# Column sums of squares accumulated by the matrix engine in the RMS norms of the third block, with four fillers ahead of the mixer

## The chip, the core and the metric

The kernel runs on one core of one Trainium2 chip. Its engines work beside each other, each through its own queue in order: the matrix engine (TensorE; PE for matmuls and PEld for weight loads in the profile), the vector engine (VectorE, DVE), the scalar engine (ScalarE, ACT), GpSimd (POOL), and SyncE (SP), which issues most of the transfers. The metric is the time of one execution on the device in microseconds (us); lower is better. Times of the profile are measured from the first instruction of the profiled execution.

## What is computed

One step of a two-layer streaming encoder, 1024 prompt positions and 64 sample positions, model width 1024, all in float32. Each layer has a mixer (layer 0: windowed attention with sinks; layer 1: a complex diagonal state-space mixer, S5, with a GLU) and a convolutional FFN of width 2816. Each of the four parts has an RMS norm ahead of it and one behind it:

```
def rms_norm(x, g):
    x32 = x.astype(jnp.float32)
    y = x32 * lax.rsqrt(jnp.mean(x32 * x32, axis=-1, keepdims=True) + NORM_EPS) * g.astype(jnp.float32)
    return y.astype(x.dtype)

for i in range(DEPTH):
    hp = rms_norm(xp, g_pre_mix[i])
    ...                                   # mixer: mp from hp
    xp = xp + rms_norm(mp, g_post_mix[i])
    hp = rms_norm(xp, g_pre_ffn[i])
    fp, cpi = conv_ffn(hp, ...)
    xp = xp + rms_norm(fp, g_post_ffn[i])
```

The sample rows (`xs`) go the same way.

## The kernel before

Activations lie transposed: the 1024 features are 8 groups (`k`) of 128 partitions, the 1088 positions are columns, cut into three blocks of 384, 384 and 320 (`BLK`; b = 0, 1, 2). Large matmuls are done as three passes of a split operand (`mm3`, lines 223 to 225: low part times high weights, high times high, high times low). Weights come from HBM as units (`raw`), are split by the scalar and vector engines (`whl`, lines 193/194 and 216) and used in a fixed order.

A norm needs, for each column, the sum of squares over all 1024 features. `rstd` (line 237) does it: the scalar engine squares two groups at a time into a buffer named by its tag (`sqa` or `sqb`, two buffers here; line 254), the vector engine adds these pairs into the first one (`acc`, line 256), then the two halves of the pair (line 260). A matmul with that 128-column piece as weights and a column of ones (scaled by 1/1024) as the moving operand then sums over the partitions, once for each of three column groups of 128 (line 266). Each such float32 matmul appears in the profile as two passes, a load and a matmul each. From the three sums the scalar engine takes a root (line 270), the vector engine a reciprocal and one Newton step (lines 271, 272, 289 to 291), and transposes on the matrix engine spread the result over the partitions (line 284). With `fine` set, which is so for the third block of a norm behind a part, the last pair is squared in two halves (line 248) and each half is added by itself (line 249).

`post_norm` (line 311 on) is the norm behind a part: squares of `y`, scaling of `y` by the gain on the scalar engine (line 320), multiplication by the spread result (line 328), addition of the residual `xl` (line 331). It runs four times for each block: behind attention (post=1), FFN 0 (post=3), the S5 mixer (post=5) and FFN 1 (post=7). Behind post=1 and post=5 follows `pre_norm`, whose outputs `hh` and `hl` (lines 300, 303 to 306) feed the FFN.

Between FFN 0 and the S5 mixer the third block takes another way, in `ssm_norm` (line 1145 on). The transposed mixer input is written to HBM unscaled (`ssm_bounce`: copies `xs` on line 1131, transfers `hd` on line 1137), read back as `U` (line 1186), and scaled later (line 1194) by `rs`, which `ssm_norm` makes of the norm's result: selection matmuls (line 1173) and two copies (lines 1175, 1176). While the squares of that block are made, the matrix engine multiplies an identity matrix by 512 columns of constants whose result nobody reads (`fill`, line 230): eight such fillers, chained by `order` one behind the other and behind the transposes of the norm before. One more filler follows the column sums and one the selection. The copies of groups 2 and 3 are ordered behind the last square.

```
            self.fill(idle, 8, 512, self.last_tr)
        ps, r = self.rstd(xt, n, "sqa" if b == 2 else "sqb", True, bcast=b < 2, ...)
```

The mixer works through 32 pairs of state groups. For each it loads parameters (`pm`, line 1213), multiplies `U` by them (lines 1249 and 1309), turns the results by `sc` (line 1257) and scans on the vector engine (lines 1280 to 1301).

The order of the instructions on each engine isn't the order in which the program issues them: a planner simulates the time line with its own costs and picks, among what is ready, what was issued first. `order(x, first)` adds an edge to it without a semaphore; `later` lowers the priority.

Of the kernel before, what the change touches and what calls it, by code (L numbers as in the profile page):

```python
# [11 lines left out]
AF = mybir.ActivationFunctionType  # L12
# [3 lines left out]
P = 128  # L16
# [27 lines left out]
class Core:  # L44
# [86 lines left out]
    sq = {}  # L131
# [79 lines left out]
    behind = ()  # L211
# [22 lines left out]
        return x  # L234


    def rstd(self, src, n, tag, root, bcast=True, first=False, alt=None, adder=None, fine=False):
        nc = self.nc
        adder = adder or nc.vector
        acc = None  # L240
        for q in range(4):
            sq = self.n2(n, tag)
            xq = src[:, 2 * q:2 * q + 2]
            if fine and q == 3:

                adder.tensor_add(acc[:, 0], acc[:, 0], acc[:, 1])
                for j in range(2):
                    nc.scalar.activation(sq[:, j], xq[:, j], AF.Square)
                    adder.tensor_add(acc[:, 0], acc[:, 0], sq[:, j])
                break  # L250
            if first:
                nc.gpsimd.tensor_mul(sq, xq, xq)
            else:
                self.sq[q] = nc.scalar.activation(sq, xq, AF.Square)
            if q:
                adder.tensor_add(acc, acc, sq)
            else:
                acc = sq
        else:
            adder.tensor_add(acc[:, 0], acc[:, 0], acc[:, 1])  # L260
        cuts = [min(c, n - P) for c in range(0, n, P)]
        nt = len(cuts)
        pr = self.sm_ps("pr", int(tag == "sqb") if alt is None else alt)
        st = pr[:, 384:384 + nt]
        for i, c in enumerate(cuts):
            self.last_st = nc.tensor.matmul(st[:, i:i + 1], acc[:, 0, c:c + P], self.ones, start=True, stop=True)
        v = self.small.tile([P, 4, 4], F32, name="nv" + tag, bufs=3)
        x, hx, r, t = (v[:, i, :nt] for i in range(4))
        if root:
            nc.scalar.activation(x, st, AF.Sqrt, bias=self.eps)  # L270
            nc.vector.tensor_scalar(hx, st, 1e-6, -0.5, op0=ALU.add, op1=ALU.mult)
            nc.vector.reciprocal(r, x)
            self.refine(r, t, hx)
        else:

            nc.vector.tensor_scalar(x, st, 1e-6, None, op0=ALU.add)
            ri = r.bitcast(I32)
            nc.vector.tensor_scalar(ri, x.bitcast(I32), 1, None, op0=ALU.logical_shift_right)
            nc.vector.tensor_scalar(hx, x, -0.5, None, op0=ALU.mult)
            nc.vector.tensor_scalar(ri, ri, -1.0, float(MAGIC), op0=ALU.mult, op1=ALU.add)  # L280
            for _ in range(3):
                self.refine(r, t, hx)
        for i, c in enumerate(cuts if bcast else []):
            self.last_tr = nc.tensor.transpose(pr[:, c:c + P], r[:, i:i + 1].to_broadcast([P, P]), self.ident)
        return pr, r
# [25 lines left out]
    def post_norm(self, y, b, g, xsrc, root, roomy, out=None, by=None):  # L311

        nc = self.nc
        n = BLK[b][1]
        xs = [self.t4([P, 2, n], "xl") if roomy and b == 2 else self.n2(n, "xl") for _ in range(4)]
        for q in range(4):
            nc.sync.dma_start(xs[q], xsrc[:, 2 * q:2 * q + 2])
        pr, _ = self.rstd(y, n, "sqa", root, alt=b % 2 if roomy else None, fine=b == 2)
        for k in range(KD):
            nc.scalar.activation(y[:, k], y[:, k], AF.Copy, scale=g[:, k:k + 1])  # L320
        V, G = nc.vector, nc.gpsimd
        by = [(G, V)[int(x)] for x in by or ("1001" if roomy and b == 2 else "0101")]

        def apply():
            last = None
            for q in range(4):
                yq = y[:, 2 * q:2 * q + 2]
                x = V.tensor_mul(yq, yq, pr[:, None, :n].to_broadcast([P, 2, n]))  # L328
                if last is not None and b == 2:
                    self.order(x, last)  # L330
                x = by[q].tensor_add(yq, yq, xs[q])  # L331
                if by[q] is V:
                    last = x
                if out is not None:
                    nc.sync.dma_start(out[:, 2 * q:2 * q + 2], yq)
        return apply
# [808 lines left out]
    def ssm_norm(self, xt, b):  # L1145

        nc = self.nc
        n = BLK[b][1]
        if b == 2:
            idle = self.mm_ps("idle")  # L1150
            self.fill(idle, 8, 512, self.last_tr)
        ps, r = self.rstd(xt, n, "sqa" if b == 2 else "sqb", True, bcast=b < 2, alt=1 - b % 2, adder=nc.gpsimd if b == 0 else None)
        if b == 0:
            jp = self.t4([P, P], "jp", I32)
            nc.gpsimd.iota(jp, pattern=[[1, P]], base=1, channel_multiplier=1)
            sel = self.t4([P, 1001], "sel")
            self.lsel, self.dsel, self.ex, self.rs, self.rn = (sel[:, x:y] for x, y in ((0, 128), (128, 144), (144, 192), (192, 233), (233, 1001)))
            nc.vector.tensor_scalar(jp, jp, 7, None, op0=ALU.bitwise_and)
            nc.vector.tensor_scalar(self.lsel, jp, 0.0, None, op0=ALU.is_equal)
            dj = self.t4([P, 16], "dj", I32)  # L1160
            nc.gpsimd.iota(dj, pattern=[[-8, 16]], base=0, channel_multiplier=1)
            nc.vector.tensor_scalar(dj, dj, 3, None, op0=ALU.arith_shift_right)
            nc.vector.tensor_scalar(self.dsel, dj, 0.0, None, op0=ALU.is_equal)
            nc.vector.memset(self.rs[:, 32:33], 0.0)
        if b < 2:
            nc.scalar.activation(self.rn[:, 384 * b:384 * b + 384], ps[:, :n], AF.Copy)
            return
        ex = self.ex
        self.fill(idle, 1, 512, self.last_st)
        for i, c in enumerate(range(0, n, P)):  # L1170
            c = min(c, n - P) // 8
            nc.vector.tensor_scalar(ex[:, 16 * i:16 * i + 16], self.dsel, r[:, i:i + 1], None, op0=ALU.mult)
            x = nc.tensor.matmul(ps[:, c:c + 16], self.lsel, ex[:, 16 * i:16 * i + 16], start=True, stop=True)
        self.fill(idle, 1, 256, x)
        nc.scalar.activation(self.rs[:, 0:32], ps[:, :32], AF.Copy)
        self.last_rs = nc.scalar.activation(self.rs[:, 33:41], ps[:, 32:40], AF.Copy)
# [423 lines left out]
```

## Time and profile before

| | |
|---|---|
| median of 3 runs | 2259.78 us (2258.66 to 2261.68) |
| the profiled execution | 2264.88 us, of which the span is 2263.1 us |
| mean granted TensorE clock | 0.990 |
| busy share of the span: PE, PEld, DVE, ACT, POOL | 97%, 94%, 75%, 45%, 18% |
| third block's norm at post=1, post=3, post=5, post=7: column sums start | 385.75, 1186.45, 1518.88, 2250.59 us |
| column sums of `ssm_norm`, third block | 1199.22 us |
| first matmul of the mixer | 1204.04 us |

In the views, a row of a time line gives start, duration, engine, line, operation, `out<-in`, form and count, and in brackets the idle time of the engine before it with what ended it. Rows of the same kind that follow each other are merged, so that a duration then covers the count behind the x.

### The profile page before, as it was taken

How to read it: one execution, taken by the hardware profiler on the slowest of the kernel's cores; microseconds unless marked ns; L12 is line 12 of the kernel's file. 1: busy time of each engine (PE TensorE's matmuls, PEld its weight loads, DVE VectorE, ACT ScalarE, POOL GpSimd, SP SyncE). 2: the span in 40 equal slices, each digit the busy share in tenths (PEclk: the TensorE clock that was granted, in tenths of full speed). 3: DMA queues.
4: the chain of work that ended last, by engine and by line, in shares of the span. 5: the costliest groups of instructions: out<-in, count | busy, mean ns of one | idle time of the engine just before them, and what ended most of it. 6: DMA issues, size and time to landing. Idle time of an engine off the chain costs nothing. (4 is left out here: it accounts for less than half of the span.)

```text
span 2263.1 us, 36074 instructions
## 1 busy us (share of the span) xinstructions
PE 2201.7 (97%) x13875; PEld 2122.4 (94%) x13875; DVE 1688.5 (75%) x2954; ACT 1019.2 (45%) x1839; POOL 415.2 (18%) x474
## 2 busy tenths in 40 slices
PE   8999999999999999999998899999999999999997
PEld 8987789999999999999996799999999999989997
DVE  8677647989877777667767855588997787686764
ACT  5255747422333343455534641263544444355543
POOL 5322004200042423000200034352011011100000
PEclk9999999999999999999998999999999999999999
DMA  5100014656345565887749888652266577578773
GB/s 195 37 21 29 16 65 151 242 191 211 107 138 185 178 203 179 259 288 222 227 164 339 262 286 300 234 166 74 96 233 218 213 287 258 193 250 278 222 256 99
DMA packets 208124, 428.48 MB, mean 189 GB/s; under 512 B 23312, under 2 KB 114224, under 8 KB 205008
## 3 DMA queue, kind: packets, MB, share of 16 engines
q1 hardware_dynamic: 175648, 326.56, 44.0%
q0 software_dynamic: 23984, 95.12, 11.6%
q10 hardware_dynamic: 8320, 4.49, 0.9%
q8 instruction: 109, 1.79, 0.3%
q14 instruction: 63, 0.52, 0.1%
HBM read 297.75 MB, written 128.37 MB: 188 GB/s over the span
## 5 line engine op out<-in xcount | busy, mean ns | idle before, releaser
L223 PE MATMUL mm<-hl,whl 128*128 128x384 f32 (+1 forms) x1960 | 643.8, 329 | 7.7 <-DVE hl L306 3.1
L225 PE MATMUL mm<-hh,whl 128*128 128x384 f32 (+1 forms) x1960 | 641.1, 328 | 2.3 <-DVE whl L216 2.3
L224 PE MATMUL mm<-hh,whl 128*128 128x384 f32 (+1 forms) x1960 | 642.2, 328 | 0.0
L223 PEld LDWEIGHTS mm<-hl,whl 128*128 128x128 f32 x1960 | 368.4, 188 | 10.8 <-DVE hl L306 4.5
L225 PEld LDWEIGHTS mm<-hh,whl 128*128 128x128 f32 x1960 | 368.4, 188 | 2.9 <-DVE whl L216 2.9
L224 PEld LDWEIGHTS mm<-hh,whl 128*128 128x128 f32 x1960 | 368.7, 188 | 0.0
L216 ACT ACTIVATE whl<-raw 128x1024 fp32r<-128x1024 f32 x202 | 212.9, 1058 | 339.1 <-PE mm L225 176.4
L216 DVE TENSOR_TENSOR whl<-raw,whl 128x1024 fp32r<-128x1024 f32 x202 | 254.4, 1263 | 96.7 <-ACT whl L216 96.2
L223 PE MATMUL mm<-gt,whl 128*128 128x384 f32 (+1 forms) x968 | 318.5, 329 | 7.9 <-DVE y L613 3.6
L225 PE MATMUL mm<-gt,whl 128*128 128x384 f32 (+1 forms) x968 | 316.9, 328 | 0.7 <-DVE whl L216 0.7
L224 PE MATMUL mm<-gt,whl 128*128 128x384 f32 (+1 forms) x968 | 317.3, 328 | 0.0
L223 PEld LDWEIGHTS mm<-gt,whl 128*128 128x128 f32 x968 | 182.9, 189 | 10.5 <-DVE y L613 4.9
L225 PEld LDWEIGHTS mm<-gt,whl 128*128 128x128 f32 x968 | 182.7, 189 | 1.0 <-DVE whl L216 1.0
L224 PEld LDWEIGHTS mm<-gt,whl 128*128 128x128 f32 x968 | 182.8, 189 | 0.0
L194 DVE TENSOR_TENSOR whl<-raw,whl 128x1024 fp32r<-128x1024 f32 x84 | 96.3, 1153 | 73.0 <-ACT whl L193 72.4
L193 ACT ACTIVATE whl<-raw 128x1024 fp32r<-128x1024 f32 x84 | 82.6, 986 | 126.8 <-DMA raw<-sd 51.0
L419 ACT ACTIVATE t<-u,ppt 128x1090 f32<-128x1090 f32 x88 | 114.2, 1298 | 50.6 <-DVE u L521 24.6
L420 DVE SCALAR_TENSOR_TENSOR t<-u,ppt,t 128x1090 f32<-128x1090 f32 x88 | 123.6, 1406 | 9.8 <-ACT t L419 9.1
L421 DVE SCALAR_TENSOR_TENSOR t<-u,ppt,t 128x1090 f32<-128x1090 f32 x88 | 123.4, 1403 | 0.4
L563 DVE TENSOR_TENSOR gt<-gr,gt 128x768 fp32r<-128x768 f32 (+2 forms) x106 | 90.2, 880 | 10.7 <-ACT gt L562 10.1
L331 POOL TENSOR_TENSOR y<-y,xl 128x768 f32<-128x768 f32 (+1 forms) x16 | 31.3, 1954 | 354.0 <-DVE y L328 288.0
L562 ACT ACTIVATE gt<-gr 128x768 fp32r<-128x768 f32 (+2 forms) x106 | 78.3, 771 | 39.5 <-DMA gr<-gd 30.2
(390 smaller groups left out, 4181.0 us busy)
## 6 DMA issues: line engine op xcount, KB each, us to landing
raw<-in_w_up SPq DMA_DIRECT2D x88, 512.0 KB, 4.3
raw<-in_w_down SPq DMA_DIRECT2D x74, 512.0 KB, 4.5
raw<-sd SPq DMA_DIRECT2D x40, 512.0 KB, 4.6
sj<-in_w_up POOLq DMA_DIRECT2D x68, 256.0 KB, 6.4
su<-sj POOLq DMA_DIRECT2D x34, 512.0 KB, 5.8
raw<-su SPq DMA_DIRECT2D x34, 512.0 KB, 4.8
pm<-prm SPq DMA_DIRECT2D x32, 522.0 KB, 8.2
gr<-td SPq DMA_DIRECT2D x40, 384.0 KB, 5.9
```

The source lines that it names most:

```text
L193: nc.scalar.activation(w[:, 0], raw, AF.Copy)
L194: nc.vector.tensor_sub(w[:, 1], raw, w[:, 0].bitcast(F32))
L216: x = nc.scalar.activation(w[:, 0], raw, AF.Copy), nc.vector.tensor_sub(w[:, 1], raw, w[:, 0].bitcast(F32))
L223: nc.tensor.matmul(out, w[:, 0, sl], xl, start=start, stop=False)
L224: nc.tensor.matmul(out, w[:, 0, sl], xh, start=False, stop=False)
L225: self.last_mm = nc.tensor.matmul(out, w[:, 1, sl], xh, start=False, stop=stop)
L331: x = by[q].tensor_add(yq, yq, xs[q])
L419: nc.scalar.activation(t, u[:, 0:T + 2], AF.Identity, bias=cb(m), scale=cw(0, m))
L420: nc.vector.scalar_tensor_tensor(t, u[:, 1:T + 3], cw(1, m), t, op0=ALU.mult, op1=ALU.add)
L421: self.last_conv = nc.vector.scalar_tensor_tensor(t, u[:, 2:T + 4], cw(2, m), t, op0=ALU.mult, op1=ALU.add)
L562: nc.scalar.activation(x[:, 0, u], raw, AF.Copy)
L563: nc.vector.tensor_sub(x[:, 1, u], raw, x[:, 0, u].bitcast(F32))
```

## The change

`rstd` takes `late`, a number of pairs, instead of `fine`. Pairs from `late` on aren't added by the vector engine: each 128 x 320 half of their squares goes to the matrix engine by itself, which accumulates the column sums in PSUM over several matmuls (`total`; the first one alone sets the start flag, the last one alone the stop flag). `late=4` is the old way. `late=3` (third block of each `post_norm`) adds the first seven groups on the vector engine as before, sums them on the matrix engine behind the last large matmul (`last_mm`), and then sums the square of the eighth group: six matmuls for three column groups instead of three. `late=0` (third block in `ssm_norm`) makes no adds at all: 24 matmuls instead of three. The PSUM tile `pr` is now taken ahead of the squares. The fillers ahead of that norm become four.

```diff
--- before.py
+++ after.py
@@ -234,20 +234,38 @@
         return x
 
 
-    def rstd(self, src, n, tag, root, bcast=True, first=False, alt=None, adder=None, fine=False):
+    def rstd(self, src, n, tag, root, bcast=True, first=False, alt=None, adder=None, late=4):
+
         nc = self.nc
         adder = adder or nc.vector
         acc = None
+        cuts = [min(c, n - P) for c in range(0, n, P)]
+        nt = len(cuts)
+        pr = self.sm_ps("pr", int(tag == "sqb") if alt is None else alt)
+        st = pr[:, 384:384 + nt]
+
+        def total(x, start, stop, behind=None):
+            for i, c in enumerate(cuts):
+                self.last_st = nc.tensor.matmul(st[:, i:i + 1], x[:, c:c + P], self.ones, start=start and i == 0, stop=stop and i == nt - 1)
+                if behind is not None:
+                    self.order(self.last_st, behind)
         for q in range(4):
             sq = self.n2(n, tag)
             xq = src[:, 2 * q:2 * q + 2]
-            if fine and q == 3:
-
-                adder.tensor_add(acc[:, 0], acc[:, 0], acc[:, 1])
+            if q >= late:
+                if q < 3:
+                    self.sq[q] = nc.scalar.activation(sq, xq, AF.Square)
                 for j in range(2):
-                    nc.scalar.activation(sq[:, j], xq[:, j], AF.Square)
-                    adder.tensor_add(acc[:, 0], acc[:, 0], sq[:, j])
-                break
+                    if q == 3:
+                        self.sq[q] = nc.scalar.activation(sq[:, j], xq[:, j], AF.Square)
+                    if late == 3 and j == 0:
+
+                        adder.tensor_add(acc[:, 0], acc[:, 0], acc[:, 1])
+                        adder.tensor_add(acc[:, 0], acc[:, 0], sq[:, j])
+                        total(acc[:, 0], True, False, self.last_mm)
+                    else:
+                        total(sq[:, j], q + j == 0, q + j == 4)
+                continue
             if first:
                 nc.gpsimd.tensor_mul(sq, xq, xq)
             else:
@@ -256,14 +274,9 @@
                 adder.tensor_add(acc, acc, sq)
             else:
                 acc = sq
-        else:
+        if late == 4:
             adder.tensor_add(acc[:, 0], acc[:, 0], acc[:, 1])
-        cuts = [min(c, n - P) for c in range(0, n, P)]
-        nt = len(cuts)
-        pr = self.sm_ps("pr", int(tag == "sqb") if alt is None else alt)
-        st = pr[:, 384:384 + nt]
-        for i, c in enumerate(cuts):
-            self.last_st = nc.tensor.matmul(st[:, i:i + 1], acc[:, 0, c:c + P], self.ones, start=True, stop=True)
+            total(acc[:, 0], True, True)
         v = self.small.tile([P, 4, 4], F32, name="nv" + tag, bufs=3)
         x, hx, r, t = (v[:, i, :nt] for i in range(4))
         if root:
@@ -315,7 +328,7 @@
         xs = [self.t4([P, 2, n], "xl") if roomy and b == 2 else self.n2(n, "xl") for _ in range(4)]
         for q in range(4):
             nc.sync.dma_start(xs[q], xsrc[:, 2 * q:2 * q + 2])
-        pr, _ = self.rstd(y, n, "sqa", root, alt=b % 2 if roomy else None, fine=b == 2)
+        pr, _ = self.rstd(y, n, "sqa", root, alt=b % 2 if roomy else None, late=3 if b == 2 else 4)
         for k in range(KD):
             nc.scalar.activation(y[:, k], y[:, k], AF.Copy, scale=g[:, k:k + 1])
         V, G = nc.vector, nc.gpsimd
@@ -1148,8 +1161,9 @@
         n = BLK[b][1]
         if b == 2:
             idle = self.mm_ps("idle")
-            self.fill(idle, 8, 512, self.last_tr)
-        ps, r = self.rstd(xt, n, "sqa" if b == 2 else "sqb", True, bcast=b < 2, alt=1 - b % 2, adder=nc.gpsimd if b == 0 else None)
+            self.fill(idle, 4, 512, self.last_tr)
+        ps, r = self.rstd(xt, n, "sqa" if b == 2 else "sqb", True, bcast=b < 2, alt=1 - b % 2, adder=nc.gpsimd if b == 0 else None,
+                          late=0 if b == 2 else 4)
         if b == 0:
             jp = self.t4([P, P], "jp", I32)
             nc.gpsimd.iota(jp, pattern=[[1, P]], base=1, channel_multiplier=1)
```

## The prediction

> **What bounds the kernel now.** I read the page first, then the chain of waits at the end, then the time line at the four places where the third block (320 columns) is normed, and the windows of the matrix engine's clock.
>
> ```profile
> span 2263.1 us, 36074 instructions
> PE 2201.7 (97%) x13875; PEld 2122.4 (94%) x13875; DVE 1688.5 (75%) x2954; ACT 1019.2 (45%) x1839; POOL 415.2 (18%) x474
> ```
> ```profile
> L266 PEld LDWEIGHTS pr<-ones,sqa x78: 186/192/192, 346.1 to 2251.1; 128*128 128x128 f32 x78
> ```
>
> The matrix engine is busy 97% of the span: what the edit can win lies in the 61 us where it isn't, and work put on it costs time wherever it is dense. The row by tile is a norm's column sum: 78 loads in 13 norms, so six passes a norm, two for each of three column groups. The profiled execution took 2264.88 us, 5.1 above the median of 2259.78 of the runs; I sum against the execution and carry the difference over to the median.
>
> The chain of waits at the kernel's end:
>
> ```profile
> 2248.93 0.50 DVE y L657
> 2249.45 0.48 ACT sqa L248
> 2249.95 0.50 DVE sqa L249
> 2250.59 0.81 PE pr L266 x6
> 2251.43 0.27 ACT nvsqa L270
> ```
>
> After the last matmul all is serial: last add, square of the last k, its add into the partial sum (L249), six passes, root. Nothing there hides a step.
>
> **The change, part by part.** *Last norm (post=7).* Removed is the second L249; the passes start behind the square. Added are six passes for the partial sum, ahead of it. Six loads take
>
> ```profile
> 2250.56 0.74 PEld L266 LDWEIGHTS pr<-ones,sqa 128*128 128x128 f32 x6 [1.93 <-issue]
> ```
>
> with 0.19 for a single one (192 ns above), so a further pass adds (0.74 - 0.19) / 5 = 0.11 us, and six in a stream 0.67. The partial sum's are ordered behind the last matmul, over by 2248.93, and the last square ends at 2249.93: 1.0 us of idle engine covers 0.74 of passes; without that cover up to 0.74 would be paid. The gain is L249's row, -0.5; bounds -0.5 and +0.2.
>
> *Norm ahead of the mixer (post=3).* The same edit, but the scalar engine stands in between:
>
> ```profile
> 1185.81 0.49 DVE L249 TENSOR_TENSOR sqa<-sqa 128x320 f32<-128x320 f32 x1 [0.63 <-ACT sqa L248]
> ```
> ```profile
> 1185.33 0.45 ACT L248 ACTIVATE sqa<-y 128x320 f32<-128x320 f32 x1
> 1186.18 0.53 ACT L1257 ACTIVATE sc<-pm 128x138 f32<-128x138 f32 x2 [0.40 <-DMA pm<-prm]
> 1186.62 0.55 ACT L320 ACTIVATE y<-y,ppt 128x320 f32<-128x320 f32 x1
> 1187.29 0.26 ACT L270 ACTIVATE nvsqa<-pr,eps 128x3 f32<-128x3 f32 x1
> ```
>
> Without L249 the sums would stand 0.5 earlier, but in today's order the root L270 queues behind L1257, which waits for a transfer until 1186.18, and L320, which ends at 1187.17. So the root comes near 1187.2: I take -0.1. Bounds: -0.5, if the root is planned ahead of L320, and 0, since the added passes find the engine idle.
>
> *Mixer entry (ssm_norm).* Removed are three pair adds (L256), one half add (L260) and four fillers; added are 48 passes in place of six. Today:
>
> ```profile
> 1188.85 8.73 PE L230 MATMUL idle<-ppt,ident 128*128 128x512 f32 x16
> ```
> ```profile
> 1190.37 0.33 PEld L230 LDWEIGHTS idle<-ppt,ident 128*128 128x128 f32 x1 [0.52 <-issue]
> 1191.22 0.33 PEld L230 LDWEIGHTS idle<-ppt,ident 128*128 128x128 f32 x1 [0.52 <-issue]
> ...
> 1195.70 0.19 PEld L230 LDWEIGHTS idle<-ppt,ident 128*128 128x128 f32 x1 [0.24 <-issue]
> 1196.13 0.19 PEld L230 LDWEIGHTS idle<-ppt,ident 128*128 128x128 f32 x1 [0.24 <-issue]
> ...
> 1199.22 0.74 PEld L266 LDWEIGHTS pr<-ones,sqa 128*128 128x128 f32 x6 [2.47 <-DVE sqa L260]
> ```
> ```profile
> 1197.81 0.83 DVE L256 TENSOR_TENSOR sqa<-sqa 128x640 f32<-128x640 f32 x1 [0.80 <-ACT sqa L254]
> 1198.67 0.49 DVE L260 TENSOR_TENSOR sqa<-sqa 128x320 f32<-128x320 f32 x1
> ```
> ```profile
> 1197.05 0.74 ACT L254 ACTIVATE sqa<-y 128x640 f32<-128x640 f32 x1 [0.89 <-DVE sqa L256]
> 1197.69 2.47 ACT L1131 ACTIVATE xs<-y 128x512 f32<-128x512 f32 x4
> 1200.09 0.26 ACT L270 ACTIVATE nvsqa<-pr,eps 128x3 f32<-128x3 f32 x1
> ```
>
> A filler is two passes (16 rows for eight), 0.85 us each early (1190.37 to 1191.22) and 0.43 late (1195.70 to 1196.13). Of 16 passes in 8.73 us, 4.4 were slow (4.4 x 0.85 + 11.6 x 0.43 = 8.73). Four fillers are 4.4 x 0.85 + 3.6 x 0.43 = 5.3, and end at 1194.1. Then 48 x 0.11 = 5.3 us of sums run to 1199.4, where today's six end at 1200.0. The squares have two buffers, so the fourth pair waits for the second's passes: 1194.1 + 24 x 0.11 = 1196.7, against 1197.05 today; in two halves of 0.46 (L248's price) it ends at 1197.7, as now (1197.79). Ordered behind it are the copies L1131, 2.47 us, to 1200.2, and today's root came right at their end. So 3 x 0.83 + 0.49 = 3.0 us of adds leave the vector engine, and the root still comes at 1200.1: next late are the matrix engine and the scalar engine's copies. I take 0. Lower bound: -0.6, if the root is planned ahead of the copies (1199.4 for 1200.0). The four fillers taken out cost nothing today: 1188.85 + 8.73 = 1197.6 lies 1.6 us before the sums. The transfers out of the copies (hd), and with them the loads of U, stand in SP's queue behind L1131 and move with it, so not at all.
>
> Edits without a price: the PSUM tile is taken ahead of the squares, but its first writer is still a pass behind them; the accumulation flags alone differ for the other norms, whose passes stay six.
>
> How much of a shift reaches the mixer's end?
>
> ```profile
> PE p L1249 <- DMA pm<-prm: 4.8, 5, 2.1
> ```
> ```profile
> 1217.44 0.69 PE L1249 MATMUL p<-U,pm 128*64 128x137 f32 x8 [0.57 <-DMA pm<-prm]
> ```
>
> In the mixer the matrix engine waits five times, 4.8 us, for parameter transfers, the first time at 1217.44 for 0.57. A lag at the entry is eaten there first, and a gain is partly turned into such a wait; so 0 is also what an uncertain entry tends to.
>
> *Norms in front of the two FFNs (post=1, post=5).*
>
> ```profile
> 379.07 0.46 DVE L249 TENSOR_TENSOR sqa<-sqa 128x320 f32<-128x320 f32 x1
> ```
> ```profile
> 402.09 0.41 PE L223 MATMUL mm<-hl,whl 128*128 128x320 f32 x1 [0.95 <-DVE hl L306]
> ...
> 410.02 0.41 PE L223 MATMUL mm<-hl,whl 128*128 128x320 f32 x1 [1.58 <-DVE hl L306]
> ```
> ```profile
> 1518.88 0.80 PE L266 MATMUL pr<-ones,sqa 128*128 128x1 f32 x6 [0.64 <-DVE sqa L249]
> ```
>
> At post=1 the vector engine is what the matrix engine waits for (0.95 and 1.58 us on L306), so an add less is worth its 0.46, and six more passes, 0.67, go into those waits. I take -0.5; bounds -0.5, and +0.7 if the passes stand in the dense part and the waits stay. At post=5 the wait of 0.64 on L249 goes and 0.67 of passes come: 0.0; bounds -0.6 and +0.7.
>
> Sum: -0.5 - 0.1 + 0 - 0.5 + 0.0 = -1.1 us. In the execution 2263.8; on the median 2259.78 - 1.1 = **2258.7**. All lower bounds together: -0.5 - 0.5 - 0.6 - 0.5 - 0.6 = -2.7.
>
> **The rivals.** *1, slower: the clock falls while the sums run.*
>
> ```profile
> 1195.87:1199.28 3.41, 1.77 (x5) 1.00 0.91 225
> 1199.28:1202.69 3.41, 2.81 (x16) 1.00 1.04 382
> 1202.69:1206.11 3.42, 2.53 (x19) 0.50 1.08 398
> 2076.51:2079.92 3.41, 1.64 (x10) 1.00 0.42 109
> 2079.92:2083.33 3.41, 3.41 (x13) 0.50 0.96 324
> ```
> ```profile
> 1206.06 1.87 PEld L1309 LDWEIGHTS p<-U,pm 128*128 128x128 f32 x8 [0.36 <-issue]
> ```
>
> (Windows cut at changes of the granted clock: width, matrix engine busy, clock.) A window with 1.77 us of fillers keeps the clock, one with 1.64 us of matmuls loses it in the next, and one with 2.81 us, in which by the code only fillers of two calls are wide and the rest are sums and selections of 1 or 16 columns, loses it too. So narrow passes hardly count, and four fillers ending at 1194.1 give their window 1.65 us: half clock from 1195.9. By then 16 passes are through; 32 are left, at a price between 0.11 (unchanged) and 0.23 (loads at half clock, 1.87 / 8). At 0.23 they end at 1203.3 instead of 1200.0: +3.2 behind 1200.1. The first transfer wait eats 0.57, so -1.1 + 2.6 = +1.5: 2261.3; with both FFN norms at +0.7 it is +3.4: 2263.2. It decides from some 10 passes at half price on (10 x 0.12 = the whole gain). Against it: where the windows fall in another execution is open, and later waits can eat more. All bounds together: +0.2 + 0 + 3.2 + 0.7 + 0.7 = +4.8.
> The Trainium skill (TensorE: Matmul & The Clock Gate, Part 1) says that the gate looks at a free-running window of 3413 ns and grants the full rate by how busy the engine has been in it. The half spells above are such windows, so the trace agrees on the length; by busy time alone, the sums would keep the clock and this rival would be out (-1.1), but the window with 2.81 busy speaks against that reading.
>
> *2, faster: the matrix engine comes free sooner.* If the clock is still full when the fillers start, or sums go between them, fillers end at 1188.85 + 8 x 0.43 = 1192.3 and the sums 1.8 us earlier, at 1197.6; with the root ahead of the copies that is -2.5, in all -3.6: 2256.2. Against it: the slow passes of today, and fillers that are chained one to the next.
>
> *3: the passes aren't hidden at the FFN norms:* +0.7 twice instead of -0.5: -0.6 + 1.4 = +0.8, 2260.6.
>
> *4: it does what it says, but the planner sets other work differently.* One more or one less of the longest transfer wait above, 2.1 us: 2256.6 to 2260.8.
>
> **How the numbers follow.** Chances: forecast 0.45, rival 1 0.22, rival 2 0.12, rival 3 0.12, rival 4 0.09. A measurement of this kernel tells 0.2%, 4.5 us, from no change. Only rival 2 or 4 with every lower bound (2259.78 - 4.5 = 2255.3) is faster by that, 0.09; only rival 1 with nothing eaten and both FFN norms paid is slower, 0.09; within, 0.82. The range takes in rival 2 and rival 1 with both FFN norms, and the 1.1 us by which the lowest of the three runs lies under the median: 2255.5 to 2263.0.
>
> **What would show it.** Right: the second L249 gone from the end's chain and the root 1.0 us behind the end of the last square, not 1.5; at the entry sums of 48 passes in one stream behind 8 filler passes, root still behind L1131; the wait at 1518.88 gone. Wrong: granted clock 0.50 in the window in which the sums run, passes 0.2 us apart, and the first mixer matmul over 1 us later than 1204 (rival 1); sums among the fillers (rival 2); new waits of the matrix engine between 380 and 415 or 1500 and 1545 (rival 3).

## The result and the profile after

The change made the kernel slower: 2268.22 us (2265.44 to 2278.6) against 2258.98 us (2258.31 to 2261.68) for the kernel before on the same chip, ratio 1.0046, 95% interval 1.0033 to 1.0058. It lies above the forecast's range (2255.5 to 2263.0). On two other chips, where the kernel before takes 2254 us, the same change gave 1.0049 (1.0035 to 1.0064) and 1.0035 (1.0022 to 1.0049).

The page of the kernel after: span, and the first line of the busy times.

```profile
span 2266.4 us, 36182 instructions
PE 2206.7 (97%) x13933; PEld 2129.3 (94%) x13933; DVE 1682.6 (74%) x2946; ACT 1017.9 (45%) x1840; POOL 414.6 (18%) x474
```

The vector engine is busy 5.9 us less (1688.5 before), the matrix engine 5.0 us more, as the edits say. The trace of before quoted in the prediction lies 5.9 us above that kernel's own median, so the two spans stand only 3.3 us apart; where they differ was therefore read from many traces (below), not from these two.

*The end.* The chain that ended last, kernel after:

```profile
2252.86 0.50 DVE y L670
2253.38 0.48 ACT sqa L260
2253.90 0.84 PE pr L249 x6
2254.77 0.27 ACT nvsqa L283
```

The second add is gone. The square ends at 2253.86 and the root starts 0.91 us later; before it was 1.50 (2249.93 to 2251.43).

*The mixer's entry.* Time line of the matrix engine, kernel after:

```profile
1189.55 5.06 PE L230 MATMUL idle<-ppt,ident 128*128 128x512 f32 x8
1194.45 5.80 PE L249 MATMUL pr<-ones,sqa 128*128 128x1 f32 x48
...
1204.37 1.87 PE L1263 MATMUL p<-U,pm 128*64 128x137 f32 x14
```

and of the scalar engine:

```profile
1197.27 0.83 ACT L260 ACTIVATE sqa<-y 128x320 f32<-128x320 f32 x2 [0.60 <-PE pr L249]
1198.00 2.45 ACT L1144 ACTIVATE xs<-y 128x512 f32<-128x512 f32 x4
1200.29 0.26 ACT L283 ACTIVATE nvsqa<-pr,eps 128x3 f32<-128x3 f32 x1
```

Eight filler passes, 48 sums in one stream, a square that waits for the sums to free its buffer, and a root that starts when both the copies and the sums are done: the entry is what the forecast drew, but for the sums, which take 5.80 us where it had 5.3. The first mixer matmul is at 1204.37, before at 1204.04.

*Where the time goes instead.* Behind the entry the matrix engine waits for parameter transfers at places where it did not before. Time line of the matrix engine, kernel after:

```profile
1217.41 2.43 PE L1263 MATMUL p<-U,pm 128*64 128x137 f32 x16 [3.79 <-DMA pm<-prm]
...
1247.29 0.69 PE L1263 MATMUL p<-U,pm 128*64 128x137 f32 x8 [1.95 <-DMA pm<-prm]
1249.90 0.69 PE L1263 MATMUL p<-U,pm 128*64 128x137 f32 x8 [1.93 <-DMA pm<-prm]
```

The first of these waits, 3.79 us where before had 0.57, is no mark of the change: over all traces of this case the waits 11 to 14 us into the mixer sum to between 0 and 3.8 us, whatever was edited. The two at 1247 and 1250, some 43 to 46 us into the mixer, have no counterpart in before, whose waits lie at 13, 34 to 35 and 54 to 55 us. In a second trace of the kernel before (run 1 below), whose mixer starts at 1199.35, the two longest are these, at 12 and 52 us:

```profile
1211.12 0.69 PE L1249 MATMUL p<-U,pm 128*64 128x137 f32 x8 [2.17 <-DMA pm<-prm]
1251.45 0.69 PE L1249 MATMUL p<-U,pm 128*64 128x137 f32 x8 [1.49 <-DMA pm<-prm]
```

In what SP issues ahead of them one thing has changed. Kernel after, time line of SP, then the scalar engine's own transfer from its time line:

```profile
1225.52 0.80 SPq L1227 DMA_DIRECT2D pm<-prm  x2
1228.88 2.62 SPq L1200 DMA_DIRECT2D U<-hd  x2
1237.42 0.33 SPq L1349 DMA_DIRECT2D yf<-yd  x1
1237.92 2.52 SPq L1227 DMA_DIRECT2D pm<-prm  x4
```
```profile
1226.21 0.38 ACTq L1344 DMA_DIRECT2D yd<-ys  x1
```

The kernel before (run 1, whose profiled execution took 2250.62 us), the same two views:

```profile
1220.80 1.77 SPq L1186 DMA_DIRECT2D U<-hd  x2
1222.68 4.61 SPq L1213 DMA_DIRECT2D pm<-prm  x2
1227.78 0.32 SPq L1335 DMA_DIRECT2D yf<-yd  x1
1228.27 2.72 SPq L1213 DMA_DIRECT2D pm<-prm  x4
```
```profile
1219.28 0.39 ACTq L1330 DMA_DIRECT2D yd<-ys  x1
```

The mixer's 32 pairs are taken two at a time, and `t` counts these steps; `U` comes in four parts, counted by `q`. The planner has set the two parameter loads of t=7 ("the pair" from here on) ahead of the two loads of U for q=2, not behind them. No line of the change touches either. Otherwise SP's order in the mixer is the same. The pair leaves just before the write of `ys`, the mixer's results, to HBM (`yd`). The load back, `yf`, waits in SP's queue until that write has landed: 8.5 us after its issue before (1219.28 to 1227.78), 11.2 us after (1226.21 to 1237.42). Four `pm` loads (t=8 and 9) stand behind `yf`; the first two of them land at 1247.15 and 1249.86, where the two new waits end. The view of the transfers, kernel after, 1215 to 1240, with the rate in 40 equal slices:

```profile
GB/s 407 388 401 421 421 414 421 394 301 227 200 271 366 371 401 389 402 439 419 405 428 427 408 411 404 350 337 229 159 152 205 121 161 231 321 325 270 191 149 302
...
pm<-prm SPq DMA_DIRECT2D x8, 522.0 KB, 11.4
```

The queues run at about 400 GB/s when the pair joins them, so by estimate it takes 2 x 522 KB / 400 GB/s = 2.6 us, near the 2.7 by which the write lands later here (11.2 - 8.5). Single traces scatter: from the write's issue to `yf` it is 7.3 to 10.0 us in the thirteen traces with the pair behind (mean 8.6; the first trace of before has 10.0) and 9.8 to 11.7 in the seven with it ahead (mean 10.8). The moment at which `yf` leaves separates them better: counted from the mixer's first matmul 28.0 to 30.6 us with the pair behind, 31.3 to 33.0 ahead; in three traces with a late entry (below), 25.8 and 26.4 behind and 28.6 ahead.

### The profile page after: what moved, and what is told of

Read it like the earlier page. It is cut to its first block, busy times and chain, and to the rows that moved or that the text cites. A ratio compares the mean times of both kernels' runs of the same rounds, so it can differ in the third digit from the quotient of the medians.

```text
span 2266.4 us, 36182 instructions
## 1 busy us (share of the span) xinstructions
PE 2206.7 (97%) x13933; PEld 2129.3 (94%) x13933; DVE 1682.6 (74%) x2946; ACT 1017.9 (45%) x1840; POOL 414.6 (18%) x474
## 3 DMA queue, kind: packets, MB, share of 16 engines
q0 software_dynamic: 23984, 95.12, 11.7%
## 5 line engine op out<-in xcount | busy, mean ns | idle before, releaser
L424 DVE TENSOR_TENSOR u<-rb,mm 128x384 f32<-128x384 f32 (+1 forms) x164 | 80.5, 503 | 22.3 <-PE mm L225 17.5
```

What stands on the lines that cost most here:

```text
L424: nc.vector.tensor_mul(u[:, t0 + 2:t0 + 2 + np_], rb[:, t0:t0 + np_], ps[:, :np_])
```

## The experiments

Three accounts were set against each other. **S**: that pair of loads costs the mixer 4 to 6 us. **B'** (B in the first runs): the entry itself does it, through later transfers and half-clock windows. **A, E, F, G, H**: the other orders that the planner changed (of the vector engine and SP in the first FFN, with post=1; of the matrix and the vector engine at the second FFN, with post=5), alone or together with the entry. Beside them stood **C**, that each edit lowers the granted clock a little, and **D**, that the loss belongs to the first runs or their chip. All ran on chips on which before takes 2253 to 2254 us; each ratio is to runs of before on the same chip, and is not always the quotient of the two medians.

Parts of the change were chosen by three constants in the kernel after; with `fine` the last square is added by the vector engine as before:

```diff
-        pr, _ = self.rstd(y, n, "sqa", root, ..., late=3 if b == 2 else 4)
+        pr, _ = self.rstd(y, n, "sqa", root, ..., late=3 if b == 2 else 4, fine=post not in POSTS)
...
-            self.fill(idle, 4, 512, self.last_tr)
+            self.fill(idle, FILLERS, 512, self.last_tr)
...
-                          late=0 if b == 2 else 4)
+                          late=ENTRY if b == 2 else 4)
```

**1. The kernel before, unchanged.**

> The kernel before, unchanged: what two copies of one program differ by, and a second trace of it. All theories: 2259 us, within 2 us of the other copy's median. The trace shown of before (2264.88) lay 5.9 above the median of its runs. If that was the clock, a trace near the median shows the shorter waits or more full-clock time between 1200 and 1550; if this trace too has 3.8 us of waits for pm in the mixer, those waits belong to every run.

Measured: 2255.19, ratio 1.0013 (1.0002 to 1.0025) to the other copy. Two copies of one program can differ by 0.13%, 2.9 us; a single figure below that says little here. Its waits for `pm` sum to 4.7 us, as in the first trace (4.8), and none lies 40 to 50 us into the mixer. What sets the two traces of before apart, 2263.1 and 2248.8 us, lies in the mixer for 3 us and in the two FFNs for 10, so a single trace doesn't give an FFN's length to within some microseconds.

**2. post=1 alone** (`POSTS=(1,)`, `ENTRY=4`, `FILLERS=8`).

> The edit at the norm ahead of the first FFN (post=1) alone; the other norms of the third block add the last square as before, the mixer's entry has its adds and eight fillers. Theory A (the planner sets the first FFN's vector and DMA work in another order, and the order costs): the norm itself is 0.5 to 1.0 us shorter, then the FFN loses 3 to 6 us, ending near 2262 (+2 to +5). Theory B (the loss comes from the mixer's entry alone, through its transfers and the clock): 2258.3, -0.5 to -1. Theory C (the loss is spread, each edit lowers the granted clock a little): +1 to +2 and a mean clock below that of before by 0.001 or more.

Measured: 2252.59, 1.0003 (0.9990 to 1.0015). A's +2 to +5 for the first FFN's new order did not come.

**3. The mixer's entry alone** (`POSTS=()`, `ENTRY=0`, `FILLERS=4`).

> The mixer's entry alone: all eight squares of the third block summed by the matrix engine, four fillers; the four norms behind the sub-layers as before. Theory A (plan): the first pair of scan parameters stands ahead of the loads of U in SP's queue, the first mixer matmul is within 0.5 us of before, and the mixer loses 2 to 4 us from 1217 on: 2261 to 2263. Theory B (transfers and clock at the entry): the whole loss, +6 to +9, 2265 to 2268. Theory of the prediction (its sums in half clock, rival 1): +1.5 to +3.2 at the first matmul of the mixer itself.

Measured: 2255.18, 1.0006 (0.9997 to 1.0015). This edit alone moves the pair of `pm`, and its mixer is long (below), yet the total hardly shows it: no theory's number was met.

**4. post=5 alone** (`POSTS=(5,)`, `ENTRY=4`, `FILLERS=8`).

> The edit at the norm ahead of the second FFN (post=5) alone. Theory A (plan): the matrix engine's and the vector engine's order behind the norm change (some 160 and 23 instructions); -0.6 to +2, and where it loses, the loss appears between 1500 and 1700 behind waits that before does not have. Theory B: 0.0 to -0.6. Theory C: +1 to +2 with a lower mean clock.

Measured: 2252.70, 0.9993 (0.9982 to 1.0004). C's +1 to +2 came neither here nor in 2.

**5. The whole change again.**

> The whole change, unchanged, once more. Parts: post=1 alone +0.03%, entry alone +0.06%, post=5 alone -0.07%, and two copies of before differ by +0.13%. Theory D (the parts add, and the first +9.2 us belong to those runs or that chip): -3 to +3 us against before, ratio 0.999 to 1.0015. Theory E (the parts together make an order that none of them has alone): +6 to +11, ratio 1.003 to 1.005. Theory B' (half-clock windows in the mixer after the entry, which fall as chance has it): +2 to +6, with a spread over 8 us between runs that follows the mean clock.

Measured: 2264.44, 1.0049 (1.0035 to 1.0064). The loss belongs to the program, not to the first chip, and it is more than the sum of the three parts, as E has it. D fell.

**6. All four norms, old entry** (`POSTS=(1,3,5,7)`, `ENTRY=4`, `FILLERS=8`).

> All four norms behind the sub-layers as in the change, the mixer's entry as before (adds and eight fillers). D: -3 to +2. E: +6 to +11 if it is post=1 with post=5, else as D. B': -2 to +1, since the entry and its transfers are as before.

Measured: 2250.16, 0.9987 (0.9977 to 0.9998).

**7. The entry with post=3, 5, 7** (`POSTS=(3,5,7)`, `ENTRY=0`, `FILLERS=4`).

> The change without post=1: the norms at post=3, 5, 7 and the mixer's entry. D: -2 to +3. E: +6 to +11 if the pair that does it is the entry with post=5, else as D. B': +2 to +6, as the whole change.

Measured: 2257.75, 1.0024 (1.0012 to 1.0035). With 6: no loss without the entry, half of it without post=1.

**8. post=3 and post=7 alone.**

> Only the norm ahead of the mixer (post=3) and the last one (post=7); nothing else of the order moves. By the prediction's steps -0.6 (the last L249 gone, -0.5, and -0.1). All theories agree: -0.6, below what the runs can tell; the trace is to show the end's root 1.0 us after the last square.

Measured: 2252.23, 0.9996 (0.9983 to 1.0008).

**9. The whole change, the pair put back.** An order edge alone:

```diff
                 for e in range(2):
                     got[t] = nc.sync.dma_start(pm[:, e], self.prm[:, 2 * t + e])
                     ...
+                    if t == 7:
+                        self.order(got[t], self.last_u)
```

> The whole change, with the one pair of scan parameters (pm of t=7) held behind the loads of U(2) in SP's queue, as it stands in before; no other engine's order moves but two rows of the vector engine. Theory S (that pair is the loss of the mixer: it delays the write of ys, behind it the load yf, and behind that the parameters of t=8 and 9): waits of 1.4 and 1.8 us for pm some 44 us into the mixer gone, the mixer 4 to 6 us shorter, 2258 to 2260 where the whole change takes 2264. Theory B' (the clock and the four fillers): no change against the whole change, 2262 to 2266.

Measured: 2259.21, 1.0020 (1.0006 to 1.0035): 5.2 below run 5, which ran on another chip.

**10. The kernel before, the pair set ahead.** The loads of U move behind it, every other engine's order stays:

```diff
                 if qs[0] == 2:
                     self.order(self.spill(), self.last_u)
-                    us.append(self.ssm_load(2))
...
                     load(t + 5, got[4])
+                    if t == 2:
+                        us.append(self.ssm_load(2))
+                        self.order(self.first_u, got[7])
+                        self.order(self.last_u, got[7])
```

> The kernel before with that pair of pm set ahead of the loads of U(2) and nothing else changed. Theory S: the same late yf and the waits for pm 44 us into the mixer, +4 to +6 us: 2258 to 2260. Theory B': within 2 us of before, 2252 to 2256.

Measured: 2259.31, 1.0020 (1.0007 to 1.0034): +5.6 by the medians, 4.5 by the ratio, with nothing of the change in it. Its SP and scalar-engine rows:

```profile
1216.70 2.17 SPq L1186 DMA_DIRECT2D U<-hd  x2
1226.32 0.33 SPq L1338 DMA_DIRECT2D yf<-yd  x1
1226.82 3.82 SPq L1213 DMA_DIRECT2D pm<-prm  x4
```
```profile
1216.48 0.39 ACTq L1333 DMA_DIRECT2D yd<-ys  x1
```

and its matrix engine, whose mixer starts at 1195.05:

```profile
1236.75 0.69 PE L1249 MATMUL p<-U,pm 128*64 128x137 f32 x8 [1.13 <-DMA pm<-prm]
1237.94 0.69 PE L1249 MATMUL p<-U,pm 128*64 128x137 f32 x8 [0.51 <-DMA pm<-prm]
```

`yf` leaves 31.3 us into the mixer, and the wait at 42 us is there. But the two waits are 1.64 us of a mixer that is 3.0 and 6.3 us longer than in the two traces of before. The longest one stands later: the scalar engine waits for another late `yf`, and the matrix engine behind it (scalar engine, then matrix engine):

```profile
1285.13 2.04 ACT L1353 ACTIVATE z<-yf 128x1024 f32<-128x1024 f32 x1 [6.02 <-DMA yf<-yd]
1289.84 1.28 PE L1312 MATMUL p<-U,pm 128*128 128x137 f32 x4 [3.85 <-ACT ys L1326]
```

That `yf`, the fifth, left 83.4 us into the mixer, in the traces of before at 80.2 and 76.8.

**11. All four norms, the pair set ahead** (6 with the edit of 10).

> All four norms, the mixer's entry as before, and that pair of pm ahead of U(2): SP's order is that of the whole change throughout. The norms alone took 2250. Theory S: +4 to +6 on that, 2254 to 2256. Theory E2 (the pair is what the norms turn from a gain to a loss of 10, through the time at which the second FFN's weights come): 2260 to 2265, as the whole change. Theory B': 2250 to 2252.

Measured: 2256.76, 1.0009 (1.0000 to 1.0019). E2 fell: the pair does not turn the norms into a loss of 10.

**12. The entry alone, the pair put back** (3 with the edit of 9).

> The mixer's entry alone (all eight squares to the matrix engine, four fillers), the pair of pm behind U(2) as in before: SP's order is that of before throughout. Entry alone with the pair ahead took 2255.2 against 2253.9. Theory S: 4 to 6 below that, 2249 to 2251. The prediction's step (entry worth 0): 2252 to 2256. Theory B': 2254 to 2257.

Measured: 2251.50, 0.9991 (0.9981 to 1.0001): 3.7 below 3, which ran on another chip. B', as far as it meant the whole loss, fell here and in 10.

**13 to 15. Which norm makes up the rest?** The kernel of 9 without post=5, without post=1, and without both.

> The whole change without post=5 (the norm ahead of the second FFN adds the last square as before), the pair of pm back behind U(2); all other orders as in the whole change with the pair back, which took 2259.2. Theory F (entry and post=5 together make the second FFN's waits for u some 5 us longer): 2252 to 2255. Theory G (post=1 with the entry): no change, 2258 to 2260.

Measured: 2254.54, 1.0010 (0.9996 to 1.0024).

> The whole change without post=1, the pair of pm back. F: 2257 to 2260, its second FFN as long as in the whole change. G: 2250 to 2254.

Measured: 2253.17, 0.9999 (0.9988 to 1.0010).

> The mixer's entry, post=3 and post=7, without post=1 and post=5, the pair of pm back: no order of the planner's is changed outside the edited lines. Both F and G: the parts add, 2250 to 2253 (entry with the pair back took 2251.5, post=3 and post=7 together -0.04%). A third theory H (the 48 passes at the entry with the earlier sums at post=3, whatever the other norms do): 2257 to 2260.

Measured: 2254.48, 0.9999 (0.9990 to 1.0009). All three stand within what two copies of before differ by. F's loss is missing in 14, H's in 15. G's 2258 to 2260 was not met in 13, but 1.0010 is too near the 1.0020 of 9 to exclude that post=1 with the entry costs something.

**16. The norms alone, again.**

> All four norms, the mixer's entry as before, once more: 2250.2 (ratio 0.9987, 95% 0.9977 to 0.9998) the first time. If that gain is real, 0.998 to 0.9995 again and 2249 to 2252; if it was chance (two copies of before differed by 1.0013), 0.9995 to 1.001.

Measured: 2253.91, 0.9999 (0.9990 to 1.0008). The gain of 6 did not come again.

**17 and 18. The whole change and the same with the pair back, side by side.**

> The whole change, unchanged, a third time: 1.0046 and 1.0049 of before so far. Both theories: 1.004 to 1.0055.

Measured: 2261.07, 1.0035 (1.0022 to 1.0049).

> The whole change with the pair of pm back behind U(2), again. Theory S alone (the pair is the whole loss): 0.999 to 1.0007 of before, some 9 to 11 us below the whole change. Theory S with a remainder (post=1 and post=5 together with the entry cost some 5 us more): 1.0015 to 1.003, some 5 us below the whole change.

Measured: 2256.42, 1.0012 (1.0000 to 1.0024): 4.7 below. With the pair back, time lines of SP and of the scalar engine:

```profile
1220.90 1.08 SPq L1200 DMA_DIRECT2D U<-hd  x2
1222.09 4.18 SPq L1227 DMA_DIRECT2D pm<-prm  x2
1226.31 0.48 SPq L1351 DMA_DIRECT2D yf<-yd  x1
1226.96 2.97 SPq L1227 DMA_DIRECT2D pm<-prm  x4
```
```profile
1218.49 0.38 ACTq L1346 DMA_DIRECT2D yd<-ys  x1
```

and the matrix engine, whose mixer starts at 1199.94; these are all its waits for `pm`:

```profile
1211.13 0.69 PE L1265 MATMUL p<-U,pm 128*64 128x137 f32 x8 [0.27 <-DMA pm<-prm]
1250.99 0.69 PE L1265 MATMUL p<-U,pm 128*64 128x137 f32 x8 [2.58 <-DMA pm<-prm]
1252.18 1.18 PE L1265 MATMUL p<-U,pm 128*64 128x137 f32 x8 [0.51 <-DMA pm<-prm]
```

`yf` leaves 26.4 us into the mixer, and nothing waits 43 us in. This is one of the traces with a late entry, though, whose mixers are short; in run 9, whose entry is on time, `yf` leaves at 29.6, no wait lies at 40 to 46 us either, and the mixer is 133.9 us long.

**The pair over all runs.** Ratio with the pair ahead less ratio with it behind, in five settings: before +0.20%; the whole change +0.26% (means of 5 and 17, of 9 and 18); entry alone +0.15%; norms alone +0.16% (11 against the mean of 6 and 16); without post=1 +0.25% (7 against 14). The mean is 0.20%, 4.6 us. Each of the five is one to two times the 0.13% of two copies, but all have one sign. The traces bear it out in place. The time from the mixer's first matmul to one fixed matmul of its output projection:

| pair of `pm` | us in each trace | mean |
|---|---|---|
| ahead (after, 3, 5, 7, 10, 11, 17) | 138.0, 135.2, 135.9, 130.8, 136.6, 136.0, 136.5 | 135.6 |
| behind (before; 1, 2, 4, 6, 8, 9, 12 to 16, 18) | 133.6; 130.3, 132.1, 131.5, 130.3, 130.5, 133.9, 132.7, 134.1, 128.9, 132.0, 130.7, 129.8 | 131.6 |

Six of the seven traces above have waits for `pm` 40 to 46 us into the mixer (0.6 to 3.9 us in sum), none of the thirteen below. Over all seven they are 2.1 us on average, half of the 4.0 by which the mixer is longer. The rest comes later. The fourth `yf` leaves 69.9 to 74.8 us into the mixer in these six, 61.5 to 66.6 in the thirteen, and only in the six does the matrix engine wait for `pm` at 80 to 85 us (0.4 to 1.4 us; runs after, 3, 5, 17) or over 3 us for the scalar engine at 94 to 95 us (runs 10, 11). That the later `yf` are late because the first was is likely, since the pair is the one thing in SP's order that differs, but it was not tested by itself. Half-clock windows, which B' has in mind, cover 16.6 us of the mixer above and 13.9 below on average: at most 1.3 us of the 4.0.

## Why the prediction was wrong

*The step that failed* is the one that costed the move of the transfers: "The transfers out of the copies (hd), and with them the loads of U, stand in SP's queue behind L1131 and move with it, so not at all." It followed the transfers that the edited code issues, not the neighbours that the planner could swap against them. That U(2) could be passed by a `pm` pair, and that `yf` blocks SP's queue until a write has landed, was nowhere priced. Rival 4 held the mechanism in words ("the planner sets other work differently"), at 2.1 us either way and a chance of 0.09. Measured, its price is 4.6 us: not one wait more but a chain, in which the pair delays the write, the write holds `yf`, `yf` holds four loads, the first two of these stop the matrix engine, and later `yf` come late too. So +4.6 where the sum had 0. The whole change lies 7.9 to 11.0 us above before (1.0035 to 1.0049), so this step is about half of the loss; the other half stays open (below).

*Last norm, -0.5:* right; the root follows the last square after 0.91 instead of 1.50 us, -0.6.

*post=3, -0.1:* right. From the last matmul ahead of the entry to this root it is 2.37 us on average in the thirteen traces with the edit and 2.59 in the seven without: -0.2.

*Entry, 0:* right on average, for a mixed reason. From that last matmul to the mixer's first it is 19.2 to 19.7 us in the nine traces with the old entry, mean 19.4. With the new one it is 18.3 to 19.3 in eight traces (mean 18.8, the lower bound of -0.6) and 20.8, 21.5 and 21.1 in three (7, 14, 18). Over all eleven the mean is 19.4, so that the 0 came out is in part luck.

*Rival 1* happened in full in these three: the sums take 7.8 to 8.1 us, against 5.4 to 6.7 in the other eight, in which the half clock comes late in the sums. Run 18, time line of the matrix engine, and windows cut where the granted clock changes:

```profile
1182.72 5.29 PE L230 MATMUL idle<-ppt,ident 128*128 128x512 f32 x8
1187.85 7.96 PE L249 MATMUL pr<-ones,sqa 128*128 128x1 f32 x48
```
```profile
1183.50:1186.92 3.42, 3.42 (x5) 1.35 (x4) 3.35 (x5) 2.42 (x5) 0.00 (x0) 0.50 0.41 167
1186.92:1190.33 3.41, 3.41 (x26) 2.86 (x25) 2.39 (x4) 2.21 (x4) 0.00 (x0) 1.00 0.88 321
1190.33:1193.75 3.42, 3.42 (x18) 3.42 (x18) 0.00 (x0) 2.98 (x6) 0.00 (x0) 0.50 0.95 285
```

The 48 passes take 7.96 us instead of 5.80 and the mixer starts 2 us later. But the forecast's "a lag at the entry is eaten" holds too: the mixers of 7, 14 and 18 are the shortest of their groups (130.8; 128.9 and 129.8). Rival 1 was no cause of the loss.

*post=1, -0.5:* not reached. 12 passes stand in one stream, and the wait of 0.95 on hl at 402 is down to 0.23 (kernel after, matrix engine):

```profile
385.82 1.39 PE L249 MATMUL pr<-ones,sqa 128*128 128x1 f32 x12
402.34 0.42 PE L223 MATMUL mm<-hl,whl 128*128 128x320 f32 x1 [0.23 <-DVE hl L319]
409.20 0.41 PE L223 MATMUL mm<-hl,whl 128*128 128x320 f32 x1 [1.90 <-DVE hl L319]
```

The next wait grew to 1.90 from 1.58. From one fixed matmul ahead of the norm to one behind both waits, the matrix engine's waits sum to 2.3 us on average in the ten traces with post=1 and to 3.0 in the ten without, a gain of 0.6 as the forecast drew. But the six passes more cost about as much, and in four of the ten (after, 6, 11, 17) a window of half clock follows at 411 to 416 us, which none of the others has there: in all 34.7 us (33.7 to 35.9) with post=1 against 34.3 (33.9 to 34.5) without, +0.4 where the sum had -0.5. Up to the end of the first FFN the ten take 2.1 us longer on average than the others (788.6 against 786.5 for one fixed pair of matmuls), but single traces run from 783 to 793, so this is not clear of their scatter.

*post=5, 0:* right as far as can be told: the wait at 1518.88 is gone, as foretold (12 passes at 1522.73 in the kernel after, without a wait), and alone it measures 0.9993.

*The range.* Its top, 2263.0, was said to take in rival 1 with both FFN norms, which the prediction put at 2263.2. It makes no difference here.

*What stays open.* With the pair back, the whole change is still at 1.0020 and 1.0012 of before, 2.7 to 4.5 us. The 2.1 us of the first FFN's new order would be about half of it or more, but they are not clear of the scatter, and kernels with post=1 and without the entry stand at 1.0003, 0.9987 and 0.9999, and copies of before differ by 0.0013. What the remainder is was not settled. Which of the entry's two edits (sums or fillers) tips the planner was not tried on the chip, and no version beat before by more than such copies differ.

## What to carry over

An edit under a planner is two changes: the instructions it names and the orders it tips elsewhere. Before costing an edit at nothing, look in the queue that feeds the next stage for a load that waits on a write's landing; what moves ahead of that write can delay all that stands behind the load, as the pair did here by some 3 us. And where two copies of a kernel differ by 0.13%, test a theory by one edge put in and taken out in several settings, and read it in the stage's own length, not in one total.

## What was not expected of the hardware

In run 18 the window from 1186.92 to 1190.33 is granted the full clock and the matrix engine is busy in all 3.41 us of it, fillers for 0.9 us and one-column sums for the rest; the next window has half. The Trainium skill (TensorE: Matmul & The Clock Gate, Part 1) says that the gate sets the rate by how busy the engine has been; by busy time as the profile counts it (matmul ends in it are modelled), this trace disagrees, since no window could be busier. The kernel after shows it without fillers: its window from 1195.76 to 1199.18 is busy for all 3.42 us with one-column sums alone, and from 1199.3 the clock is half. That passes of one column hardly count, as the prediction took from a window with 2.81 us, fits all three.
